# The channel mixer's seam: the first block's high and low parts summed once and kept for operands five and seven, with other places and orders of the passes

## The chip, the cores and the metric

The kernel runs on one core of a Trainium2 chip. The metric is the device time of one execution in microseconds (us), as the median of several runs. Engines are named as in the profile: PE (TensorE, matmuls), PEld (its weight loads), DVE (VectorE), ACT (ScalarE), POOL (GpSimd), SP (SyncE, which issues most transfers).

## The reference

Two encoder layers on 1024 tokens of width 1024; the mixers of tokens are a windowed attention in layer 0 and a gated linear recurrence in layer 1. The change touches only the channel mixer, which ends each layer:

```python
def conv_ffn(v, w_in, conv_w, conv_b, w_out):
    gate, up = jnp.split(v @ w_in, 2, axis=-1)
    hid = jax.nn.gelu(dwconv_centred(gate, conv_w, conv_b)) * up
    return hid @ w_out

def reference(x, mem, norm_g, ...):
    for layer in range(DEPTH):
        u = rmsnorm(h, norm_g[layer, 0])
        ...
        h = h + rmsnorm(y, norm_g[layer, 1])
        f = conv_ffn(rmsnorm(h, norm_g[layer, 2]), ffn_w_in[layer], ffn_conv_w[layer],
                     ffn_conv_b[layer], ffn_w_out[layer])
        h = h + rmsnorm(f, norm_g[layer, 3])
    return h
```

`v` is 1024 x 1024, `w_in` 1024 x 5632 (22 tiles of 128 gate columns and as many up columns), the convolution has width 3 along the tokens.

## The kernel before, in words

**Precision.** Each float32 operand is kept as two parts: a high part `h`, which ACT makes with a cast, and a low part `l`, which DVE makes as source minus `h` (function `split`; `nsplit` makes both with the sign turned). A product of two such operands is three matmuls per 128-deep slice: high by high, low by high, high by low.

**Seven products in place of eight.** The first matmul of the channel mixer (function `ffn`) sees its input `v` transposed as four blocks: channels 0-511 or 512-1023 by the 512 tokens of half `ti` or of half `tj`. For one tile `f` of 128 gate and 128 up columns the four block results (gate and up, each for both token halves) are formed from seven products of sums of blocks. `prod(k, ...)` runs product k: 4 slices by 3 matmuls, 12 matmuls of 128x128 by 128x512. The right-hand operands are `B[1]` to `B[7]`. `B[1]`, `B[2]`, `B[3]` and, at first, `B[5]` are the four blocks themselves, high and low (`uh`, `ul`). The others are sums, made once for each layer by `operands()`, in halves of 128x1024: x = block 1 - block 5 becomes operand five in place; x + block 3 gives operand six (`nsplit`); that minus block 1 gives operand seven; x (of six) minus block 2 gives operand four. Since a block lies there as high and low part, adding or subtracting it takes two DVE passes (helper `more`), so a layer's operands take 18 passes beside the splits: 6 for five, 4 each for six, seven and four.

The left-hand operands are sums of weight blocks, which transfers that add on the way into SRAM build (`load`: buffers `st`, `sx`, `sy`; the refill of `sy` waits until DVE has read the old one) and `weights` splits into `wh` and `wl`.

**The seam.** The operands aren't ready when the first matmul can start, so `first_units()` begins with tile 0 by plain products of the four blocks (`plain`, banks X, Y, V), and takes tiles 1 and 2 together: products 1 and 2 of both, then 5, 3, 6, 7, 4, each of both tiles before the next, in step with the operands as they get done. X, V and Y are accumulation banks, two of each; `su`, `s5`, `s` are copies of banks that ACT makes, and `u`, `g` are the up and gate results that `conv` takes. From tile 3 on the order is regular, and all operands lie there. The seam stands once in each layer: at about 560 to 640 us in layer 0, and at about 1985 to 2080 us in layer 1.

**What sets the order.** The kernel is written as a program of tiles; a scheduler puts the instructions on each engine's queue by priority, as their inputs come to be placed, and adds the semaphore waits. `tc.high_priority(AHEAD)` draws instructions forward by 2000 places, `tc.issue_after(x)` holds one back until x has been placed. Engines run their queues strictly in that order. Before the change only operand seven's passes are drawn forward.

## Time and profile before

| | us |
|---|---|
| median of 3 runs | 2633.48 |
| the runs | 2632.31, 2633.48, 2636.83 |
| profiled execution, its own time | 2636.21 |
| its span in the profile | 2634.4 |
| PE busy | 2594.2 (98%), 14372 matmuls |
| PEld busy | 2180.0 (83%) |
| DVE busy | 1753.5 (67%) |
| ACT busy | 1400.6 (53%) |
| POOL busy | 471.7 (18%) |

The profile shows one execution; the span is what lies between its first and last instruction. Busy PE time is not PE at its best: a matmul that starts late because the one before runs at a lower clock counts as busy. A timeline row reads: start (us), duration (us), engine, line, operation, output<-inputs, shape, count, and in square brackets the wait ahead of it and what ended the wait. L584 is the matmul in `mmk`, L85 the cast and L86 the subtraction of `split`, L607 and L608 those of `nsplit`, L663 the pass of `more`, L670 to L672 the passes of operand five, L808 and L824 the additions that make `u`, L788, L815 and L823 the copies `s`, `s5` and `su`.

### The profile page before, as it was taken

Reading aid. Unit: us, or ns where it says so; the run is one execution under the profiler, and the core shown is the slowest. Engines: PE = TensorE matmul, PEld = TensorE weight load, DVE = VectorE, ACT = ScalarE, POOL = GpSimd, SP = SyncE. Lnnn points to the kernel's source line nnn. Section 1 sums busy time; section 2 is a strip of 40 time slices with the busy share of each in tenths; the row PEclk is TensorE's granted clock in tenths of the full one; section 3 lists DMA queues with packets and bytes.
Section 4 is the critical chain, followed back from the end, with each engine's and each line's share of the span. In section 5 each row is a group of like instructions: output and inputs, shape, how many; then the busy total and the mean of one; then the engine's idle time right before and its main releaser. Section 6 shows DMA issues by size and latency. Waiting matters only on the chain.

```text
span 2634.4 us, 38871 instructions
## 1 busy us (share of the span) xinstructions
PE 2594.2 (98%) x14372; PEld 2180.0 (83%) x14372; DVE 1753.5 (67%) x2852; ACT 1400.6 (53%) x2534; POOL 471.7 (18%) x520
## 2 busy tenths in 40 slices
PE   8999999999999999999999999999999999999998
PEld 7988888888888888887888878888887788888887
DVE  6778777587656565487587575867657665656447
ACT  6667767445444444465465564646434444444453
POOL 0421110221111100032133131221311111110013
PEclk9999999999999999999999999999999999999999
DMA  9782232467877756683236241113337777775666
GB/s 357 248 191 47 75 114 61 130 186 189 214 198 200 199 155 221 220 274 124 85 122 172 81 112 41 61 49 97 122 112 200 199 198 199 203 200 170 202 210 232
DMA packets 195726, 425.92 MB, mean 162 GB/s; under 512 B 20048, under 2 KB 56272, under 8 KB 189904
## 3 DMA queue, kind: packets, MB, share of 16 engines
q1 hardware_dynamic: 161552, 324.06, 37.7%
q0 software_dynamic: 24544, 90.19, 16.5%
q10 hardware_dynamic: 9440, 9.19, 1.1%
q8 instruction: 113, 1.85, 0.3%
q14 instruction: 77, 0.63, 0.1%
HBM read 330.04 MB, written 116.39 MB: 169 GB/s over the span
## 4 chain that ended last, share of the span: by engine, by line
PE 90%; DVE 5%; DMA 2%; ACT 1%; issue 1%; POOL 0%; SPq 0%; DVEq 0%; ACTq 0%; POOLq 0%
PE X L584 29%; PE V L584 10%; PE pj L80 8%; PE pj L82 8%; PE pj L81 8%; PE Y L584 5%; PE pb L80 4%; PE pb L81 4%; PE pb L82 4%; PE po L1302 2%; PE pa L1221 1%; PE pt L386 1%; PE pu L1280 1%; PE po L390 1%; DMA sx<-in_ffw_dram 1%
## 5 line engine op out<-in xcount | busy, mean ns | idle before, releaser
L86 DVE TENSOR_TENSOR wl<-st,wh 128x1024 fp32r<-128x1024 f32 (+1 forms) x238 | 262.7, 1110 | 321.8 <-ACT wh L85 295.2
L85 ACT CAST wh<-st 128x1024 fp32r<-128x1024 f32 (+1 forms) x238 | 222.5, 936 | 286.5 <-PE X L584 179.8
L80 PE MATMUL pj<-uh,wh 128*128 128x512 f32 x512 | 204.1, 399 | 1.2 <-DVE q L1140 0.8
L584 PE MATMUL X<-wl,wh 128*128 128x512 f32 x528 | 204.9, 390 | 0.2 <-DVE wl L86 0.2
L584 PE MATMUL X<-wh,wl 128*128 128x512 f32 x528 | 204.9, 389 | 0.0
L81 PE MATMUL pj<-ul,wh 128*128 128x512 f32 x512 | 202.9, 396 | 0.0
L82 PE MATMUL pj<-uh,wl 128*128 128x512 f32 x512 | 202.3, 395 | 0.0
L584 PE MATMUL X<-wh 128*128 128x512 f32 x528 | 198.7, 390 | 0.6 <-DVE c L1014 0.6
L80 PE MATMUL pj<-wh,uh 128*128 128x384 f32 (+1 forms) x512 | 188.4, 369 | 1.0 <-DVE v L298 1.0
L82 PE MATMUL pj<-wh,ul 128*128 128x384 f32 (+1 forms) x512 | 187.2, 366 | 0.0
L81 PE MATMUL pj<-wl,uh 128*128 128x384 f32 (+1 forms) x512 | 186.9, 365 | 0.0
L76 DVE TENSOR_TENSOR wl<-st,wh 128x1024 fp32r<-128x1024 f32 (+1 forms) x90 | 115.5, 1288 | 24.1 <-ACT wh L75 22.8
L584 PE MATMUL V<-uh,wh 128*128 128x512 f32 x336 | 130.7, 389 | 0.0
L584 PE MATMUL V<-ul,wh 128*128 128x512 f32 x336 | 130.7, 389 | 0.0
L584 PE MATMUL V<-uh,wl 128*128 128x512 f32 x336 | 130.7, 389 | 0.0
L584 PEld LDWEIGHTS X<-wh 128*128 128x128 f32 x528 | 99.1, 188 | 21.7 <-issue 1.0
L584 PEld LDWEIGHTS X<-wl,wh 128*128 128x128 f32 x528 | 99.1, 188 | 21.3 <-DVE wl L86 0.7
L584 PEld LDWEIGHTS X<-wh,wl 128*128 128x128 f32 x528 | 99.1, 188 | 20.4
L75 ACT CAST wh<-st 128x1024 fp32r<-128x1024 f32 (+1 forms) x96 | 96.6, 1012 | 34.9 <-PE pj L81 20.0
L80 PEld LDWEIGHTS pj<-uh,wh 128*128 128x128 f32 x512 | 96.8, 189 | 20.4 <-DVE q L1140 1.2
L973 POOL TENSOR_TENSOR c<-c,g 128x512 f32<-128x512 f32 x24 | 43.2, 1818 | 389.4 <-PE X L584 320.1
L82 PEld LDWEIGHTS pj<-uh,wl 128*128 128x128 f32 x512 | 96.8, 189 | 19.3
(410 smaller groups left out, 7161.1 us busy)
## 6 DMA issues: line engine op xcount, KB each, us to landing
st<-hid SPq DMA_DIRECT2D x154, 256.0 KB, 3.3
st<-in_ffw_dram SPq DMA_DIRECT2D x108, 256.0 KB, 3.3
w2s<-in_ffw_dram POOLq DMA_DIRECT2D x24, 1024.0 KB, 8.5
st<-in_ffw_dram SPq DMA_DIRECT2D x46, 512.0 KB, 4.5
hid<-tt SPq DMA_DIRECT2D x88, 256.0 KB, 4.9
st<-w2s SPq DMA_DIRECT2D x88, 256.0 KB, 3.3
sx<-in_ffw_dram SPq DMA_DIRECT2D x84, 256.0 KB, 3.9
sy<-in_ffw_dram SPq DMA_DIRECT2D x42, 512.0 KB, 6.3
```

The costliest lines, as they stand in the source:

```text
L75: act.copy(h[:, :n], raw)
L76: (eng or dve).tensor_tensor(l[:, :n], raw, h[:, :n].bitcast(F32), op=ALU.subtract)
L80: pe.matmul(o, ah, bh, start=first, stop=False)
L81: pe.matmul(o, ah, bl, start=False, stop=False)
L82: return pe.matmul(o, al, bh, start=False, stop=last)
L85: act.copy(h, src)
L86: return dve.tensor_tensor(l, src, h.bitcast(F32), op=ALU.subtract)
L386: pe.transpose(tp[:, j, :], sm[:, j, c * P:(c + 1) * P], ident)
L390: pe.matmul(po, v[:, lo + c, :], pl, start=False, stop=c == hi - lo - 1)
L584: last = pe.matmul(o, x, y, start=first and i == 0, stop=i == len(ops) - 1, skip_group_check=not first)
L973: pool.tensor_tensor(y[q][:, t, :], y[q][:, t, :], g3[:, c], op=ALU.mult)
L1302: pe.matmul(po[:, c, :], x, y, start=i == 0, stop=i == len(ops) - 1)
```

## The change

In `operands`, the high and low part of block 1 are added once for each half into a buffer `whole`, which stays. Operand five becomes whole minus the two parts of block 5 (6 passes, as before), and operand seven one pass for each half, x - whole, in place of two: 16 passes in place of 18. The two sums take the two `tt` buffers until operand seven is split in place there; so the `u` of tile 2 moves from a `tt` buffer to the `g` buffer, and the `g` of both tiles take the `tt` buffers.

The rest sets orders. Operand six's splits are held until the last pass of tile 0's convolution has been placed (`wide[0]`, L616 after the change). Operand seven's subtractions are held until tile 1's `u<-Y` has been placed (`ups[0]`, now L814), its splits until tile 2's. Operand four's passes are held until the last low part of operand seven (`low7`). The splits of the second and third weight parts are held until operand five, and operand six, are split (`made5`). Lines move: L584 is now L583, the two lines of `split` are one, L85, `more` is L665, the passes of operand five L672 to L674, operand seven's L686, `u<-Y` L814, `u<-V` L831.

```diff
--- before.py
+++ after.py
@@ -82,8 +82,7 @@
         return pe.matmul(o, al, bh, start=False, stop=last)
 
     def split(h, l, src):
-        act.copy(h, src)
-        return dve.tensor_tensor(l, src, h.bitcast(F32), op=ALU.subtract)
+        return act.copy(h, src), dve.tensor_tensor(l, src, h.bitcast(F32), op=ALU.subtract)
 
     def rstd_of(pl, ss, n, count, tag):
         ms = pl.tile([P, n], F32, tag=tag + "ms", name=tag + "ms")
@@ -604,15 +603,18 @@
             B[k] = tuple(u2p.tile([P, 4, 512], F32R, name=f"u{k}{c}") for c in "hl")
         def nsplit(h, l_, src):
 
-            act.activation(h, src, AF.Copy, scale=-1.0)
-            dve.scalar_tensor_tensor(l_, src, -1.0, h.bitcast(F32), op0=ALU.mult, op1=ALU.subtract)
+            return (act.activation(h, src, AF.Copy, scale=-1.0),
+                    dve.scalar_tensor_tensor(l_, src, -1.0, h.bitcast(F32), op0=ALU.mult, op1=ALU.subtract))
+
+        wide = []
 
         def conv(f, g, u):
 
             c = fp.tile([P, T], F32, tag="c", bufs=3, name="c")
             act.activation(c, g, AF.Identity, bias=cb[:, f:f + 1], scale=ncw[:, f, 1:2])
             dve.scalar_tensor_tensor(c[:, 1:], g[:, :T - 1], ncw[:, f, 0:1], c[:, 1:], op0=ALU.mult, op1=ALU.add)
-            dve.scalar_tensor_tensor(c[:, :T - 1], g[:, 1:], ncw[:, f, 2:3], c[:, :T - 1], op0=ALU.mult, op1=ALU.add)
+            wide.append(dve.scalar_tensor_tensor(c[:, :T - 1], g[:, 1:], ncw[:, f, 2:3], c[:, :T - 1],
+                                                 op0=ALU.mult, op1=ALU.add))
             act.activation(c, c, AF.Gelu_apprx_tanh)
             dve.tensor_tensor(c, u, c, op=ALU.mult)
             return c
@@ -653,7 +655,7 @@
                 act.copy(u[:, m], up_)
             yield conv(f, g, u)
 
-        def operands(made5):
+        def operands(made5, ups):
 
             xs = [fp.tile([P, 2, 512], F32, tag="c", bufs=3, name="c") for _ in range(2)]
             tmp = lambda: fp.tile([P, 2, 512], F32, tag="tt", bufs=2, name="tt")
@@ -664,27 +666,31 @@
                     x = o
             def out_of(sp, k, kk, x):
                 return sp(half(B[k][0], kk), half(B[k][1], kk), x)
-            for kk, x in enumerate(xs):
-                q = tmp()
+            whole = [tmp() for _ in xs]
+            for kk, (x, q) in enumerate(zip(xs, whole)):
                 f32 = lambda t, c: half(t[c], kk).bitcast(F32)
-                dve.tensor_tensor(x, f32(B[1], 0), f32(B[5], 0), op=ALU.subtract)
-                dve.tensor_tensor(q, f32(B[1], 1), f32(B[5], 1), op=ALU.subtract)
-                dve.tensor_tensor(x, x, q, op=ALU.add)
+                dve.tensor_tensor(q, f32(B[1], 0), f32(B[1], 1), op=ALU.add)
+                dve.tensor_tensor(x, q, f32(B[5], 0), op=ALU.subtract)
+                dve.tensor_tensor(x, x, f32(B[5], 1), op=ALU.subtract)
             for kk, x in enumerate(xs):
                 made5.append(out_of(split, 5, kk, x))
             yield
             for kk, x in enumerate(xs):
                 more(x, x, B[3], kk, ALU.add)
-                out_of(nsplit, 6, kk, x)
+            for kk, x in enumerate(xs):
+                with tc.issue_after(wide[0].ins):
+                    made5.append(out_of(nsplit, 6, kk, x))
+            yield
+            for kk, (x, q) in enumerate(zip(xs, whole)):
+                with tc.high_priority(AHEAD), tc.issue_after(ups[0].ins):
+                    dve.tensor_tensor(q, x, q, op=ALU.subtract)
+            for kk, q in enumerate(whole):
+                with tc.high_priority(AHEAD), tc.issue_after(ups[1].ins):
+                    low7 = out_of(split, 7, kk, q)[1]
             yield
             for kk, x in enumerate(xs):
-                q = tmp()
-                with tc.high_priority(AHEAD):
-                    more(q, x, B[1], kk, ALU.subtract)
-                    out_of(split, 7, kk, q)
-            yield
-            for kk, x in enumerate(xs):
-                more(x, x, B[2], kk, ALU.subtract)
+                with tc.issue_after(low7.ins):
+                    more(x, x, B[2], kk, ALU.subtract)
                 out_of(split, 4, kk, x)
             yield
 
@@ -789,8 +795,8 @@
 
 
             tiles = (1, 2)
-            made5 = []
-            pl, opd = plain(0), operands(made5)
+            made5, ups = [], []
+            pl, opd = plain(0), operands(made5, ups)
             next(pl)
             raws = {f: load(f) for f in tiles}
             gens = {f: weights(raws.pop(f)) for f in tiles}
@@ -804,16 +810,17 @@
                 start(us[f])
                 y = psx.tile([P, 512], F32, tag="Y", name="Y")
                 prod(2, operand(us[f], 2), y, True)
-                us_[f] = fp.tile([P, T], F32, tag="u" if f == 1 else "tt", bufs=1 if f == 1 else 2, name="u")
-                dve.tensor_tensor(us_[f][:, ti], y, s[1], op=ALU.add)
-            with tc.issue_after(made5[-1].ins):
+                us_[f] = fp.tile([P, T], F32, tag="u" if f == 1 else "g", bufs=1, name="u")
+                ups.append(dve.tensor_tensor(us_[f][:, ti], y, s[1], op=ALU.add))
+            with tc.issue_after(made5[1][0].ins), tc.issue_after(made5[1][1].ins):
                 more_of()
             for f in tiles:
                 vs[f] = psx.tile([P, 512], F32, tag="V", name="V")
                 prod(5, operand(us[f], 5), vs[f], True)
                 s5[f] = fp.tile([P, 512], F32, tag="s5" if f == 1 else "s1", bufs=1, name="s5")
                 act.copy(s5[f], vs[f])
-            more_of()
+            with tc.issue_after(made5[3][0].ins), tc.issue_after(made5[3][1].ins):
+                more_of()
             next(opd)
             for f in tiles:
                 prod(3, operand(us[f], 3), vs[f], False)
@@ -828,7 +835,7 @@
             gen = weights(raws.pop(3))
             for f, x in zip(tiles, X):
                 prod(7, operand(us[f], 7), x, False, f == 1)
-                gs[f] = gtile() if f == 1 else fp.tile([P, T], F32, tag="tt", bufs=2, name="tt")
+                gs[f] = fp.tile([P, T], F32, tag="tt", bufs=2, name="tt")
                 act.copy(gs[f][:, tj], x)
                 dve.tensor_tensor(gs[f][:, tj], gs[f][:, tj], s5[f], op=ALU.add)
                 ops.append(next(gen))
```

The order of DVE (VectorE) in layer 1 around operand seven, before; `tt` is operand seven ahead of its split, `c` in `more` (L663) operand four, u7l and u4l the low parts:

```order
L86 TENSOR_TENSOR wl<-sy,wh 128x1024
L808 TENSOR_TENSOR u<-Y,s_19291 128x512
L808 TENSOR_TENSOR u<-Y,s_19321 128x512
L663 TENSOR_TENSOR tt<-c,uh 128x1024
L663 TENSOR_TENSOR tt<-tt,ul 128x1024
L663 TENSOR_TENSOR c<-c,uh 128x1024
L86 TENSOR_TENSOR wl<-st,wh 128x512
L824 TENSOR_TENSOR u<-V,su 128x512
L86 TENSOR_TENSOR u7l<-tt,u7h 128x1024
L663 TENSOR_TENSOR c<-c,ul 128x1024
L663 TENSOR_TENSOR tt<-c,uh 128x1024
```

And with the change:

```order
L85 TENSOR_TENSOR wl<-sy,wh 128x1024
L814 TENSOR_TENSOR u<-Y,s_19287 128x512
L686 TENSOR_TENSOR tt<-c,tt 128x1024 x2
L814 TENSOR_TENSOR u<-Y,s_19317 128x512
L85 TENSOR_TENSOR u7l<-tt,u7h 128x1024
L85 TENSOR_TENSOR wl<-st,wh 128x512
L831 TENSOR_TENSOR u<-V,su 128x512
L85 TENSOR_TENSOR u7l<-tt,u7h 128x1024
L665 TENSOR_TENSOR c<-c,uh 128x1024 x2
L665 TENSOR_TENSOR c<-c,ul 128x1024 x2
L831 TENSOR_TENSOR u<-V,su 128x512
L85 TENSOR_TENSOR wl<-st,wh 128x512
```

Both halves of operand seven are now subtracted and split ahead of every pass of operand four; before, a pass of operand four stood between the halves' passes. Ahead of these rows, the last pass of tile 0's convolution and both of operand six's low parts now stand ahead of both `wl<-sy` passes; before, one of those stood ahead of them. The two kept sums `tt<-uh,ul` (L672) stand ahead of the last `wl` and `ul` passes of the layer's norm, where before nothing of the operands stood.

ACT (ScalarE) in layer 1 at the same place, before; u7h and u4h are the high parts:

```order
L85 CAST u7h<-tt 128x1024
L823 COPY su<-X 128x512
L85 CAST wh<-st 128x512
L85 CAST u4h<-c 128x1024
L85 CAST u7h<-tt 128x1024
L85 CAST u4h<-c 128x1024
L832 COPY g<-X 128x512
```

And with the change:

```order
L85 CAST u7h<-tt 128x1024
L821 COPY s_19370<-V 128x512
L830 COPY su<-X 128x512
L85 CAST wh<-st 128x512
L85 CAST u4h<-c 128x1024
L839 COPY tt<-X 128x512
L85 CAST u4h<-c 128x1024
```

The u7h row of the first fence is the first half's, with the second half's behind the first u4h; in the second fence the u7h row is already the second half's, ahead of the copy `su`; both u4h casts now stand behind tile 2's `wh<-st` cast.

PE in layer 1 where tile 2's first product (X_19308 before, X_19304 now) begins behind tile 1's, with buffer numbers, before; V and `qin` belong to tile 0's plain product:

```order
L584 MATMUL X_19278<-uh_77,wl_19237 128x512
L584 MATMUL X_19308<-uh_77,wh_19240 128x512
L584 MATMUL X_19308<-ul_78,wh_19240 128x512
L584 MATMUL V_19085<-uh_77,qin0_18436 128x512
L584 MATMUL Y_19086<-uh_77,wh_19031 128x512
L584 MATMUL Y_19293<-uh_77,wh_19236 128x512
```

And with the change:

```order
L583 MATMUL X_19304<-uh_77,wh_19236 128x512
L583 MATMUL X_19304<-ul_78,wh_19236 128x512
L583 MATMUL X_19304<-uh_77,wl_19237 128x512
L583 MATMUL X_19304<-uh_77,wh_19236 128x512
L583 MATMUL X_19304<-ul_78,wh_19236 128x512
L583 MATMUL X_19304<-uh_77,wl_19237 128x512
```

The rows left out with the change are six more of the product's 12 matmuls and then V; before, two of the 12 stood ahead of V, and the other ten later.

## The prediction

> **What bounds the kernel now.** First the page's head and the table of busy times, then the table of waits of TensorE (PE), because only time in which PE stands still or runs slowly can be won here: the change moves passes of DVE and ACT and leaves all matmuls in.
>
> ```profile
> span 2634.4 us, 38871 instructions
> PE 2594.2 (98%) x14372; PEld 2180.0 (83%) x14372; DVE 1753.5 (67%) x2852; ACT 1400.6 (53%) x2534; POOL 471.7 (18%) x520
> ...
> engine line waited for: us in total, times, longest us
> PE X L584 <- ACT u7h L85: 3.8, 1, 3.8
> PE X L584 <- ACT wh L85: 0.9, 1, 0.9
> PE X L584 <- DVE u7l L86: 0.5, 1, 0.5
> PE V L584 <- ACT uh L85: 0.2, 1, 0.2
> ```
>
> PE is busy for 98%. The rows with L584 are all the waits that it has in the two channel mixers, 5.4 us, and all four lie in the seams. Two of them are for operand seven: 3.8 us in layer 1, 0.5 us in layer 0. So the timeline of PE there, layer 1 first, then layer 0, then one window with the granted clock (0.86, behind the busy times of PE, PEld, DVE, ACT and POOL):
>
> ```profile
> 2039.09 0.39 PE L584 MATMUL X<-u7h,wl 128*128 128x512 f32 x1
> 2039.32 0.39 PE L584 MATMUL X<-u7h,wh 128*128 128x512 f32 x1
> 2039.54 0.39 PE L584 MATMUL X<-u7l,wh 128*128 128x512 f32 x1
> 2039.77 0.39 PE L584 MATMUL X<-u7h,wl 128*128 128x512 f32 x1
> 2043.98 0.80 PE L584 MATMUL X<-u7h,wh 128*128 128x512 f32 x1 [3.83 <-ACT u7h L85]
> 2044.58 0.63 PE L584 MATMUL X<-u7h,wl 128*128 128x512 f32 x1
> 2045.00 0.63 PE L584 MATMUL X<-u7h,wh 128*128 128x512 f32 x1
> ...
> 2048.84 0.39 PE L584 MATMUL X<-u4h,wh 128*128 128x512 f32 x1
> ...
> 610.73 0.39 PE L584 MATMUL X<-u7h,wl 128*128 128x512 f32 x1
> ...
> 614.90 0.98 PE L584 MATMUL X<-u7l,wh 128*128 128x512 f32 x3 [0.45 <-DVE u7l L86]
> ...
> 616.64 0.40 PE L584 MATMUL X<-u4h,wh 128*128 128x512 f32 x1
> ...
> 2037.00:2049.00 12.00, 8.18 (x29) 6.33 (x29) 10.89 (x12) 4.82 (x6) 2.63 (x3) 0.86 0.61 131
> ```
>
> Undisturbed starts stand (2039.77 - 2039.09) / 3 = 0.227 us apart. From 2039.77 to 2048.84 PE starts 15 matmuls, 15 x 0.227 = 3.40 us of work in 9.07: **5.67 us** lost. 3.98 of it is the wait, and 1.69 comes behind it, where starts are 0.43 apart (2044.58, 2045.00) and the window's clock falls to 0.86. In layer 0, 21 starts from 610.73 to 616.64 are 4.76 us in 5.91: **1.15 us**. The most that operand seven can give is 6.82 us.
>
> [...]
>
> Why operand seven is late, the queue of DVE shows:
>
> ```profile
> 2029.22 0.68 DVE L808 TENSOR_TENSOR u<-Y,s 128x512 f32<-128x512 f32 x1
> ...
> 2033.56 1.22 DVE L663 TENSOR_TENSOR c<-c,uh 128x1024 f32<-128x1024 f32 x1
> ...
> 2038.17 1.22 DVE L663 TENSOR_TENSOR tt<-c,uh 128x1024 f32<-128x1024 f32 x1
> ...
> 2041.64 1.22 DVE L663 TENSOR_TENSOR tt<-tt,ul 128x1024 f32<-128x1024 f32 x1
> 2042.77 1.22 DVE L663 TENSOR_TENSOR c<-c,uh 128x1024 f32<-128x1024 f32 x1
> ...
> 2042.89 1.04 ACT L85 CAST u7h<-tt 128x1024 fp32r<-128x1024 f32 x1 [3.56 <-DVE tt L663]
> ```
>
> DVE works without a pause from 2031 to 2046. The second half of operand seven (tt, 2038.17 and 2041.64) queues behind passes of operand four (c, from 2033.56), and its cast ends at 2043.93, where PE goes on. It is the order on DVE, not its amount of work, that PE waits for.
>
> **The change part by part.** *Passes.* Operand five takes 6 passes as before, seven 2 in place of 4, by the kept sums: 16 in place of 18 in each layer. A pass takes 1.22 us, and a start follows 1.13 behind another (2041.64 to 2042.77). So DVE loses 2 x 1.13 = 2.3 us per layer, worth nothing in itself off PE's path.
>
> *The kept sums* now stand ahead of the seam on DVE. In layer 0, and behind it in layer 1, DVE has holes:
>
> ```profile
> 571.88 0.69 DVE L86 TENSOR_TENSOR ul<-pt,uh 128x512 fp32r<-128x512 f32 x1 [2.92 <-ACT uh L85]
> ...
> 1993.87 1.28 DVE L86 TENSOR_TENSOR ul<-pt,uh 128x512 fp32r<-128x512 f32 x2
> 2001.50 1.23 DVE L86 TENSOR_TENSOR wl<-st,wh 128x1024 fp32r<-128x1024 f32 x1 [6.35 <-ACT wh L85]
> ...
> 1997.32 1.03 PE L117 MATMUL pt<-ident,nu 128*128 128x128 f32 x8
> ```
>
> Two sums, 2.27 us, fit into 2.92 and 6.35. In layer 1 they push the two ul halves from 1993.87-1995.15 to 1997.42; the transposes pt that need their bank stand at 1997.32, but now with four more X matmuls ahead, at 1998.2. Cost 0, cover 0.8 us; without that cover it would be up to 2.27.
>
> *Seven ahead of four.* From 2029.22 on DVE now does: u (0.6), both subtractions (2.27), u, u7l, wl, u, u7l, then four passes of operand four. So both tt are whole at 2029.8 + 2.4 = 2032.2, ACT has the second u7h by about 2034.6 (behind wh, su and the first u7h), and DVE the second u7l by 2036.3. PE, which now does the second tile's V product behind the first tile's seven, asks for u7h's second half at about 2036.2: 1.6 us to spare, where it was 4 late. I take the whole 6.82 us back.
>
> *What is late next* is operand four. PE comes to it at 2048.84 - 5.67 = 2043.2 (2043.5 with the loss below). Its four passes now stand from 2036.3 to 2040.8 on DVE, but its casts stand on ACT behind one that waits for PE:
>
> ```profile
> 2037.70 0.62 ACT L85 CAST wh<-st 128x512 fp32r<-128x512 f32 x1 [1.04 <-PE V L584]
> 2038.28 1.05 ACT L85 CAST u4h<-c 128x1024 fp32r<-128x1024 f32 x1
> ```
>
> That V product of the second tile now ends at about 2040.3, the wh cast at 2040.9, u4h at 2041.9, u4l (1.22, behind u and wl) at 2043.5, and the second matmul of operand four wants it at 2043.7. The two meet within 0.2 us; layer 0 has the same order and the same distance. Bounds: 0, and 2.0 for both seams (each cast behind the wait late by one more cast, 1.05); I take 0.3, nearer to 0, since the rows leave it just on time.
>
> *The second tile's first product* stands whole ahead of V in PE's queue in layer 1 (12 matmuls; before, 2):
>
> ```profile
> 2000.42 1.04 ACT L85 CAST wh<-st 128x1024 fp32r<-128x1024 f32 x1 [7.51 <-DMA st<-in_ffw_dram]
> 2001.52 0.50 PE L584 MATMUL X<-uh,wh 128*128 128x512 f32 x1 [0.88 <-ACT wh L85]
> 2001.85 0.40 PE L584 MATMUL X<-ul,wh 128*128 128x512 f32 x1
> 2002.49 0.50 PE L584 MATMUL V<-uh,qin 128*128 128x512 f32 x1 [0.24 <-ACT uh L85]
> ```
>
> The wait of 0.88 stays: as many matmuls stand ahead of it, and the load is issued as before. The third matmul now reads wl, which DVE ends at 2001.50 + 1.23 = 2002.73; V went on at 2002.49. Cost 0.3 us; bounds 0 (another order of ends) and 0.5.
>
> *The other orders*, issue constraints, the u of tile two in the buffer of g and both g in tt cost PE nothing that a row shows: their passes keep their number and PE has no other wait here. The refill of the shared weights is later; that is the third rival.
>
> Sum: -6.82 + 0.3 + 0.3 = **-6.2 us**. The profiled execution took 2636.21 us (span 2634.4), 2.7 above the median of the runs shown, 2633.48, and inside their range (2632.31 to 2636.83). From its time the sum makes 2630.0; from the median, which is what is asked for, 2633.5 - 6.2 = 2627.3.
>
> **Rivals.**
> *Operand four is late by as much as a cast on ACT.* The bound above: 2.0 in place of 0.3 gives -4.5 us, 2629.0. For it: the wait at ACT's head and the margin of 0.2. Against: PE now has other matmuls (V, Y of tile three) mixed in there.
>
> *The slow stretch is not in the median run.* The 1.69 us behind the wait hang on the clock falling to 0.86. If a run of median time has the wait without it, the gain is 6.2 - 1.7 = 4.5 us: 2629.0 too. For it: the profiled run lies 2.7 above the median. Against: the wait of 3.83 is itself long, and the spread may come from elsewhere. [...]
>
> *Slower: the refill of the shared weights.* The wl<-sy pass, which frees the buffer sy for tile three's load, now stands behind STT and both u6l passes on DVE, 1.19 + 2 x 1.13 = 3.5 us later, and SP, POOL and POOL follow in a chain:
>
> ```profile
> 2023.31 0.33 SPq L700 DMA_DIRECT2D sy<-in_ffw_dram  x1
> 2032.70 0.89 POOL L703 DMA_DIRECT2D sy<-sx  x1 [1.10 <-DVE tt L663]
> 2038.37 0.88 POOL L704 DMA_DIRECT2D sy<-sy  x1 [4.79 <-DMA sy<-sx]
> 2051.53 1.05 ACT L85 CAST wh<-sy 128x1024 fp32r<-128x1024 f32 x1 [0.66 <-PE X L584]
> ...
> DMA to landing us min/median/max: 3.3/5.1/9.6
> ```
>
> Moved by 3.5, the last add starts at 2041.9 and lands, 5.1 later, at 2047.0; ACT wants it at 2051.53 - 5.4 = 2046.1 and has the copies that free PE's bank X behind it, with some 3 us until PE asks for that bank. From 4 us of further delay PE waits one for one; with all three transfers at 9.6 it is 13.5 later, PE waits some 9.5, and 9.5 - 6.2 makes it 3 slower; slower by over 5.3 us needs two such seams: 2640. Against it: the queue rows keep gaps, and two passes are saved.
>
> *The change does not bring seven forward*: then only the 0.3 is left, 2633.8. The order on DVE speaks against it: nothing of operand four stands ahead of u7l.
>
> **How the numbers follow.** Forecast 0.52; operand four late 0.15; no slow stretch in the median 0.22; seven not forward or part of it 0.06; slower 0.05. What can be told from no change is 0.2%, 5.3 us, so faster means below 2628.2. The forecast's own spread (its costs at 0 to 2.5 together, and a median that moves by about 1) runs from 2625 to 2630; of its 0.52 I count 0.41 below 2628.2, and 0.10 of the two cases at 2629.0 (each could be half as large). Faster 0.51, same 0.44, slower 0.05. Predicted 2627.3; range 2623 to 2633: below, 6.82 without costs (2626.7) and some 4 for the spread of the runs, which lie 4.5 apart; above, the two rivals at 2629.0 and the same 4.
>
> **What would show it.** Right: no wait of PE for u7h or u7l in either seam, clock 1.00 in the windows of layer 1, both tt<-c,tt passes back to back behind the first u<-Y. The wait for wh at the second tile's first product still there, near 0.9, with one of about 0.6 for wl behind it. Waits of PE for u4h, u4l or the copy of X: below 0.3 each if my sum holds, about 1 if the first rival does. A wait for wh<-sy or for X's bank in tile three would show the slower case. The forecast is wrong if the waits are gone and the time is not: then the median runs never held them in full.

## The result, and the profile after

The changed kernel takes 2629.75 us in the median of 16 runs (2626.55 to 2635.04), the kernel before, in the same comparison, 2634.07 us (16 runs). The ratio is 0.9979 with a 95% interval of 0.9973 to 0.9986: some 5.5 us faster, between 3.7 and 7.1. The forecast was 6.2 us and 2627.3.

The profiled execution took 2631.85 us. The head of its page, and all waits of PE between 1975 and 2100 us (engine, line, what it waited for: us in total, times, longest); the same view between 560 and 660 us is empty:

```profile
span 2630.1 us, 38871 instructions
PE 2593.0 (99%) x14372; PEld 2179.7 (83%) x14372; DVE 1747.6 (66%) x2848; ACT 1400.2 (53%) x2534; POOL 470.2 (18%) x520
```

```profile
PE X L583 <- ACT wh L85: 2.0, 1, 2.0
PE X L583 <- DVE wl L85: 0.5, 1, 0.5
```

DVE has four instructions fewer: the two saved passes in each layer. No wait for operand seven is left, and none for operand four. The timeline of DVE in layer 1, then ACT, then PE, shows why:

```profile
2030.37 2.35 DVE L686 TENSOR_TENSOR tt<-c,tt 128x1024 f32<-128x1024 f32 x2
2032.64 0.68 DVE L814 TENSOR_TENSOR u<-Y,s 128x512 f32<-128x512 f32 x1
...
2035.58 1.21 DVE L85 TENSOR_TENSOR u7l<-tt,u7h 128x1024 fp32r<-128x1024 f32 x1
2036.71 2.35 DVE L665 TENSOR_TENSOR c<-c,uh 128x1024 f32<-128x1024 f32 x2
...
2042.71 1.22 DVE L85 TENSOR_TENSOR u4l<-c,u4h 128x1024 fp32r<-128x1024 f32 x1
...
2034.46 1.05 ACT L85 CAST u7h<-tt 128x1024 fp32r<-128x1024 f32 x1
...
2041.11 0.62 ACT L85 CAST wh<-st 128x512 fp32r<-128x512 f32 x1 [4.17 <-PE V L583]
2041.63 1.04 ACT L85 CAST u4h<-c 128x1024 fp32r<-128x1024 f32 x1
...
2036.15 0.39 PE L583 MATMUL X<-u7h,wh 128*128 128x512 f32 x1
...
2044.53 0.39 PE L583 MATMUL X<-u4l,wh 128*128 128x512 f32 x1
```

Both halves of `tt` are whole at 2032.72, the second u7h at 2035.51, and PE is in operand seven from 2036.15 without a pause; its fifth matmul, at 2036.15 + 4 x 0.227 = 2037.06, is the first that reads the second u7h. Operand four's u4h is ready at 2042.67 and u4l at 2043.93, 0.6 us ahead of the matmul that reads it.

What is left is at the start of layer 1's seam, where the second tile's first product waits for its weights and then runs slowly. PE's timeline there, and the windows view of two stretches (the seventh figure is the granted clock):

```profile
1998.36 0.39 PE L583 MATMUL X<-uh,wl 128*128 128x512 f32 x1
2000.75 0.50 PE L583 MATMUL X<-uh,wh 128*128 128x512 f32 x1 [2.00 <-ACT wh L85]
...
2002.01 0.50 PE L583 MATMUL X<-uh,wl 128*128 128x512 f32 x1 [0.53 <-DVE wl L85]
...
2003.47 0.63 PE L583 MATMUL X<-uh,wh 128*128 128x512 f32 x1
2003.89 0.63 PE L583 MATMUL X<-ul,wh 128*128 128x512 f32 x1
...
2005.99 0.40 PE L583 MATMUL V<-uh,qin 128*128 128x512 f32 x1
```

```profile
2000.50:2006.00 5.50, 4.73 (x13) 3.43 (x14) 5.27 (x6) 2.15 (x5) 0.86 (x1) 0.69 1.03 291
2035.00:2050.00 15.00, 15.00 (x67) 12.08 (x66) 13.49 (x15) 7.36 (x11) 2.71 (x4) 1.00 0.80 183
```

From 1998.36 to 2005.99 PE starts 13 matmuls, 13 x 0.227 = 2.95 us of work in 7.63: 4.7 us lost. In the kernel before, this place lost 1.7 (the waits of 0.88 and 0.24 and a slower start behind each). A run of starts 0.43 us apart, nearly twice the 0.227 between undisturbed ones, is called a slow stretch below; the granted clock of 0.69 in the first window shows it (0.51 from 2002.6 to 2006.0 alone, 0.50 from 2043.9 to 2047.2 in the first profile of before).

### The profile page after: what moved, and what is told of

The parts are those of the page before. It is cut to its first block, busy times and chain, and to the rows that moved or that the text cites. A ratio compares the mean times of both kernels' runs of the same rounds, so it can differ in the third digit from the quotient of the medians.

```text
span 2630.1 us, 38871 instructions
## 1 busy us (share of the span) xinstructions
PE 2593.0 (99%) x14372; PEld 2179.7 (83%) x14372; DVE 1747.6 (66%) x2848; ACT 1400.2 (53%) x2534; POOL 470.2 (18%) x520
## 4 chain that ended last, share of the span: by engine, by line
PE 92%; DVE 4%; DMA 2%; ACT 1%; issue 1%; POOL 0%; SPq 0%; ACTq 0%; DVEq 0%; POOLq 0%
PE X L583 30%; PE V L583 11%; PE pj L80 8%; PE pj L82 8%; PE pj L81 8%; PE Y L583 5%; PE pb L80 4%; PE pb L82 4%; PE pb L81 4%; PE po L1309 2%; PE pt L385 1%; PE pa L1228 1%; PE pu L1287 1%; PE po L389 1%; PE pt L116 1%
## 5 line engine op out<-in xcount | busy, mean ns | idle before, releaser
L85 DVE TENSOR_TENSOR wl<-st,wh 128x1024 fp32r<-128x1024 f32 (+1 forms) x238 | 262.8, 1111 | 319.4 <-ACT wh L85 301.6
L85 ACT CAST wh<-st 128x1024 fp32r<-128x1024 f32 (+1 forms) x238 | 222.4, 936 | 290.5 <-PE X L583 178.0
L583 PE MATMUL X<-wl,wh 128*128 128x512 f32 x528 | 204.9, 390 | 0.2 <-DVE wl L85 0.2
L583 PE MATMUL X<-wh,wl 128*128 128x512 f32 x528 | 204.9, 389 | 0.0
L583 PE MATMUL X<-wh 128*128 128x512 f32 x528 | 198.7, 390 | 0.6 <-DVE c L1021 0.6
L583 PE MATMUL V<-uh,wh 128*128 128x512 f32 x336 | 130.8, 389 | 0.0
L583 PE MATMUL V<-ul,wh 128*128 128x512 f32 x336 | 130.7, 389 | 0.0
L583 PE MATMUL V<-uh,wl 128*128 128x512 f32 x336 | 130.7, 389 | 0.0
L583 PEld LDWEIGHTS X<-wh 128*128 128x128 f32 x528 | 99.1, 188 | 21.7 <-issue 1.0
L583 PEld LDWEIGHTS X<-wl,wh 128*128 128x128 f32 x528 | 99.1, 188 | 21.1 <-DVE wl L85 0.7
L583 PEld LDWEIGHTS X<-wh,wl 128*128 128x128 f32 x528 | 99.1, 188 | 20.6
```

The costliest lines, as they stand in the source:

```text
L85: return act.copy(h, src), dve.tensor_tensor(l, src, h.bitcast(F32), op=ALU.subtract)
L583: last = pe.matmul(o, x, y, start=first and i == 0, stop=i == len(ops) - 1, skip_group_check=not first)
```

## The experiments

All runs were compared with runs of the kernel before on the same chip. Beside the time stands a measure from the one profile that each kernel left: how much longer than 0.2275 us the starts of PE lie apart, summed over all that are more than 0.26 apart, from 555 to 660 and from 1975 to 2100 us of the profile. It is PE's loss in the two seams. The names are those of the runs: order_only has the orders without the kept sums, sums_only the sums without the constraints, ups_only only the two constraints on operand seven, gate_only operand four held behind seven, buf_only the buffers alone, sums_behind the sums later, and a1 stands for the early load.

| kernel | median us (runs) | ratio to before, 95% | PE's loss in the seams, us |
|---|---|---|---|
| before, first profile | 2634.07 (16) | | 8.9 |
| before_again | 2636.00 (12) | 1.0004 (0.9994 to 1.0013) | 11.1 |
| changed | 2629.75 (16) | 0.9979 (0.9973 to 0.9986) | 5.4 |
| after_again | 2628.89 (11) | 0.9976 (0.9967 to 0.9985) | 4.9 |
| order_only | 2627.20 (8) | 0.9978 (0.9968 to 0.9988) | 2.5 |
| sums_only | 2638.32 (11) | 1.0013 (1.0004 to 1.0022) | 12.0 |
| ups_only | 2628.64 (7) | 0.9975 (0.9965 to 0.9985) | 3.4 |
| gate_only | 2634.00 (11) | 0.9999 (0.9990 to 1.0008) | 8.1 |
| buf_only | 2636.51 (11) | 1.0013 (1.0004 to 1.0022) | 12.5 |
| sums_behind | 2627.92 (11) | 0.9977 (0.9968 to 0.9986) | 2.4 |
| before_a1 | 2634.90 (11) | 0.9998 (0.9990 to 1.0007) | 9.1 |
| a1_first | 2624.84 (5) | 0.9963 (0.9951 to 0.9976) | 0.8 |
| a1_again | 2626.24 (5) | 0.9965 (0.9953 to 0.9977) | 0.9 |
| order_a1 | 2629.63 (11) | 0.9983 (0.9974 to 0.9992) | 2.5 |

Against the mean of the two profiles of before, 10.0, the loss explains every ratio within about 3 us; so the effect lies in the seams, as far as these times can tell.

### Both kernels once more

No edit. For the changed kernel:

> The changed kernel once more. Theory E (the wait for tile 2's first weights and the slow stretch behind it come in every run): a wait of 0.9 to 2.0 us for wh, one near 0.5 for wl, then 6 to 10 starts that are 0.43 apart. Rival F (the slow stretch is there in some runs only): the same waits, but no or few starts above 0.3. No wait for u7h, u7l, u4h or u4l above 0.3 in either case. Time 0.1 to 0.3% below before.

Waits of 1.76 and 0.53 us came again, with a slow stretch behind them from about 2001 to 2004.2, and no wait for operands seven or four. For the kernel before:

> The kernel before once more. Theory K (the slow stretch behind the 3.8 us wait is part of what the change takes away in every run): wait for u7h 3.7 to 3.9, then at least 4 starts that are 0.43 apart. Rival L (it is there in some runs only): the same wait with starts 0.23 apart behind it, so that operand seven is worth 1.5 less than in the first profile. Waits of 0.5 for u7l in layer 0 and of 0.8 to 1.1 for wh in layer 1 in either case.

The first seam stall was longer this time, the wait for u7h shorter. PE's timeline:

```profile
2002.88 0.50 PE L584 MATMUL X<-uh,wh 128*128 128x512 f32 x1 [1.34 <-ACT wh L85]
...
2003.86 0.55 PE L584 MATMUL V<-uh,qin 128*128 128x512 f32 x1 [0.24 <-ACT uh L85]
...
2045.78 0.80 PE L584 MATMUL X<-u7h,wh 128*128 128x512 f32 x1 [2.64 <-ACT u7h L85]
```

Theory K holds in these profiles as to the slow stretch: it is there, and it is longer (13 starts 0.43 apart, to 2051.92; in the first profile 6). But the wait for u7h was 2.64, not the 3.7 to 3.9 that both theories expected. PE had lost 3.7 us at the seam's start (1.6 of waits and a slow stretch), 2.0 more than in the first profile, and waited 1.2 less at operand seven: the two stalls aren't independent. PE won nothing by that here: with the longer slow stretch behind it, operand seven cost 5.8 us in layer 1, against 5.7 in the first profile. The next run shows the dependence more cleanly.

### The early load, on the kernel before

```diff
-            raws = {f: load(f) for f in tiles}
+            a1s = {f: first_load(f) for f in tiles}
+            raws = {f: load(f, a1s[f]) for f in tiles}
```

`first_load` allocates the staging buffer of a tile's first weights and issues their load; `load` no longer does.

> The kernel before, with tile 2's first weights loaded early as in the faster version of the changed kernel, and nothing else. Theory C (the load is a loss of its own): the waits of 0.9 for wh and 0.2 for uh at the seam's start go, 1.0 to 1.5 us faster than before; the waits of 3.8 and 0.5 for operand seven stay. Rival M (PE then only comes earlier to operand seven): the wait for u7h grows by what the start has saved, 4.5 to 5 us, and the time stays within 0.5 us of before.

All waits of PE in layer 1's seam:

```profile
PE X L584 <- ACT u7h L85: 5.4, 1, 5.4
```

PE at its first matmul into Y and where operand seven goes on; the first row is the kernel before, the others the kernel with the early load:

```profile
1991.30 0.47 PE L584 MATMUL Y<-uh,wh 128*128 128x512 f32 x1
```

```profile
1989.19 0.47 PE L584 MATMUL Y<-uh,wh 128*128 128x512 f32 x1
...
2041.91 0.80 PE L584 MATMUL X<-u7h,wh 128*128 128x512 f32 x1 [5.38 <-ACT u7h L85]
```

Rival M is right in direction: the waits at the start are gone, and the wait for u7h has grown from 3.8 to 5.4 (it said 4.5 to 5), by what the start had saved. Operand seven goes on 52.7 us after the first matmul into Y in both profiles (1991.30 to 2043.98 before), whether PE lost 1.7 us at the seam's start or nothing. In before_again, with 3.7 lost, it was 53.6; whether the larger loss held the chain up isn't shown. The ratio of the times, 0.9998, agrees, though its interval alone would leave room for the 1.0 to 1.5 us of theory C. In these two profiles operand seven comes when the chain on DVE and ACT has made it, and since that chain ends last, the 1.7 us that PE lost ahead of it were free.

### The early load, on the changed kernel

The same edit on the changed kernel, run twice.

> The changed kernel, but tile 2's first weight load is issued directly behind tile 1's first load, and takes the staging buffer that tile 1's last load took; no other edit. Theory C (what the changed kernel still loses at the start of layer 1's seam is this load: wait for wh 2.0, for wl 0.5, then 8 starts that are 0.43 apart, 1.6 us): all three are gone, 4.1 us less than the changed kernel's profiled run, 2.5 to 4.5 less in the median. Rival D (V and the transposed halves are late anyway, as the wait of 0.24 for uh before V shows): the wait moves to V<-uh, 1.5 to 2 us of it stay, gain below 2 us.

> The changed kernel with the early load once more, for its interval: 3.5 to 5 us faster than the changed kernel (0.9955 to 0.997 of before), no wait of PE in the channel mixers' seams above 0.3.

SP, ACT and PE of the first of them (tile 2's load is the second of the two on SP; its wh cast is the row of ACT; the last row is V behind the whole product), then PE's windows over the seam, of the kernel before, the changed one and this one:

```profile
1971.35 9.57 SPq L700 DMA_DIRECT2D st<-in_ffw_dram  x2
...
1988.07 1.06 ACT L85 CAST wh<-st 128x1024 fp32r<-128x1024 f32 x1
...
1996.94 0.40 PE L583 MATMUL X<-uh,wh 128*128 128x512 f32 x1
...
1998.99 0.40 PE L583 MATMUL V<-uh,qin 128*128 128x512 f32 x1
```

```profile
1975.00:2080.00 105.00, 100.06 (x442) 81.64 (x442) 78.59 (x87) 48.99 (x66) 16.18 (x20) 0.98 0.74 198
```

```profile
1975.00:2080.00 105.00, 102.47 (x453) 83.58 (x452) 75.67 (x85) 48.23 (x66) 16.15 (x20) 0.98 0.75 201
```

```profile
1975.00:2080.00 105.00, 105.00 (x472) 86.44 (x471) 79.00 (x85) 53.37 (x71) 16.43 (x20) 1.00 0.76 199
```

Theory C holds: the weights are cast at 1988, PE runs from the first product into V and on, and is busy for all of the 105 us with a granted clock of 1.00. On the changed kernel the edit is worth 4.0 to 4.6 us by the seams' loss, where on the kernel before it was worth nothing. The two ratios, 0.9963 and 0.9965 of before (some 9.5 us), lie 3 to 4 us below those of the changed kernel, with intervals that overlap a little; this is the fastest version of the study.

### The orders without the kept sums

```diff
-                dve.tensor_tensor(q, f32(B[1], 0), f32(B[1], 1), op=ALU.add)
-                dve.tensor_tensor(x, q, f32(B[5], 0), op=ALU.subtract)
-                dve.tensor_tensor(x, x, f32(B[5], 1), op=ALU.subtract)
+                dve.tensor_tensor(x, f32(B[1], 0), f32(B[5], 0), op=ALU.subtract)
+                dve.tensor_tensor(q, f32(B[1], 1), f32(B[5], 1), op=ALU.subtract)
+                dve.tensor_tensor(x, x, q, op=ALU.add)
...
-                    dve.tensor_tensor(q, x, q, op=ALU.subtract)
+                    more(q, x, B[1], kk, ALU.subtract)
```

> The changed kernel's orders and buffers, with the 18 passes of before: block 1 is not summed ahead, operand seven takes four passes again. Theory A (the order on DVE is what PE waited for): no wait of PE for u7h or u7l above 0.7 us in either seam, against 3.8 and 0.5 before, since both halves of operand seven still stand ahead of operand four. Rival B (the two saved passes are what counts): the wait for u7h comes back with 2 us or more. Under A the two passes that are not saved (2.27 us on DVE) should show one step later, at operand four: its last low part, which had 0.2 to 0.6 us to spare, comes 1 to 2 us late in layer 1, so the kernel is 1 to 2.5 us slower than the changed one and still 2 to 4 faster than before.

PE's waits in layer 1's seam (layer 0's has none):

```profile
PE Y L583 <- ACT wh L85: 0.5, 1, 0.5
PE V L583 <- ACT wh L85: 0.5, 1, 0.5
PE X L583 <- ACT u4h L85: 0.2, 1, 0.2
```

Theory A holds: no wait for operand seven with all 18 passes. Where operand four is due there are waits of 1.2 us, 0.2 of them for operand four itself and the rest for weights cast beside it on ACT. The kernel was expected to be slower than the changed one and is not: its seams lose 2.4 to 2.9 us less. At the start of layer 1's seam it has no wait, since the scheduler puts V and Y of the plain tile ahead of tile 2's first product, and its weights are cast by then:

```profile
1996.49 1.05 ACT L85 CAST wh<-st 128x1024 fp32r<-128x1024 f32 x1 [2.10 <-DMA st<-in_ffw_dram]
...
1996.23 0.40 PE L583 MATMUL V<-uh,qin 128*128 128x512 f32 x1
```

This order at the start isn't due to the missing sums alone: the kernel before has none either and puts two matmuls of tile 2's product ahead of V, and the runs with the buffers alone and with operand four held back, told of below, have V first as well. The scheduler moves this place with edits made elsewhere. So by the waits the sums save some 1.2 us at operand four; what they cost at the start this run can't tell.

### The sums without the constraints

The changed kernel with every `issue_after` that it brought taken out again (here the pair at operand seven; each half's subtraction and split then stand together again, in one loop):

```diff
-                with tc.high_priority(AHEAD), tc.issue_after(ups[0].ins):
+                with tc.high_priority(AHEAD):
                     dve.tensor_tensor(q, x, q, op=ALU.subtract)
...
-                with tc.high_priority(AHEAD), tc.issue_after(ups[1].ins):
-                    low7 = out_of(split, 7, kk, q)[1]
+                    out_of(split, 7, kk, q)
```

> The changed kernel with the kept sums, 16 passes and the new buffers, but without every constraint on the order (operand six, seven and four and the two weight splits are held behind nothing new). The passes of seven are then drawn forward ahead of both u<-Y additions. Theory A (the constraints matter): u<-Y of tile 1 comes some 4 us later, the copy s of tile 2 on ACT waits for it, and PE waits 2 to 6 us in a place where it waited for nothing in the changed kernel (for u7h, V or Y); time within 2 us of before. Rival B (sums and buffers are enough): seams as in the changed kernel, time within 1 us of it.

PE's largest waits over both seams:

```profile
PE X L583 <- ACT s L789: 3.4, 2, 1.7
PE X L583 <- ACT su L824: 2.5, 3, 1.0
PE X L583 <- ACT wh L85: 2.1, 1, 2.1
PE V L583 <- ACT s L816: 0.7, 1, 0.7
```

Slower than before: 1.0013. Operand seven is early, but its passes, drawn forward, push `u<-Y` back; the copies s and su come late, and PE waits for the banks that these have to empty. Theory A's mechanism holds, and more strongly than it said: 6.6 us of such waits over both seams in place of 2 to 6, and 3.4 us slower than before (1.1 to 5.8) where it said within 2.

### The sums with only the two constraints on operand seven

The kernel just told of, with `issue_after(ups[0])` and `issue_after(ups[1])` put back.

> The changed kernel with the kept sums and the new buffers, and of all constraints only the two that hold operand seven's subtractions and splits behind the u<-Y additions. Theory H (these two are what the kernel with the sums alone lacked): no wait for the copies s and su; the second half's u7l, with three more passes ahead of it on DVE, comes 3.4 us later than in the changed kernel, where it had 1.6 to spare, so a wait of 1 to 2 us for u7l in layer 1; 0.5 to 2.5 us slower than the changed kernel and faster than before. Rival N (the constraints on operands six and four are needed too): waits for su, s or u4 of over 2 us come back.

PE's waits in layer 1's seam (layer 0's has one of 0.3 us):

```profile
PE X L583 <- ACT wh L85: 1.2, 1, 1.2
PE X L583 <- DVE wl L85: 0.5, 1, 0.5
```

As fast as the changed kernel (0.9975). Theory H is right about the waits for s and su, and too dark about u7l: the wait of 1 to 2 us didn't come, and the kernel isn't slower than the changed one. Of all constraints these two are enough, as far as an interval of 2.6 us to each side can tell.

### The buffers alone, and the order alone

The kernel before, with the two buffers exchanged and nothing else:

```diff
-                us_[f] = fp.tile([P, T], F32, tag="u" if f == 1 else "tt", bufs=1 if f == 1 else 2, name="u")
+                us_[f] = fp.tile([P, T], F32, tag="u" if f == 1 else "g", bufs=1, name="u")
...
-                gs[f] = gtile() if f == 1 else fp.tile([P, T], F32, tag="tt", bufs=2, name="tt")
+                gs[f] = fp.tile([P, T], F32, tag="tt", bufs=2, name="tt")
```

> The kernel before with nothing but the two buffers exchanged: tile 2's u in the g buffer, both g in the tt buffers. 18 passes, no constraint on the order. Rival G (the buffer was the cause): both halves of seven can be made at once, waits for u7h gone. Theory H (the buffer frees seven, but with no constraint the passes drawn forward push both u<-Y additions back, as in the kernel with the sums alone, where PE waited 3.4 us for the copy s and 2.5 for su): waits for s and su of 4 to 8 us in the two seams together, 2 to 7 us slower than before. Both may hold: then the buffers are needed and the constraints too.

PE's waits over both seams:

```profile
PE X L584 <- ACT su L823: 3.4, 4, 1.8
PE X L584 <- ACT u7h L85: 2.3, 1, 2.3
PE X L584 <- ACT s L788: 1.2, 1, 1.2
```

Theory H holds: waits of 4.6 us for s and su, and slower than before. Rival G's waits for u7h aren't gone: one of 2.3 us stays, since a pass of operand four still stands between operand seven's on DVE. So the buffers alone are not enough. The kernel before, with operand four held behind operand seven and nothing else:

```diff
-                    out_of(split, 7, kk, q)
+                    low7 = out_of(split, 7, kk, q)
...
-                more(x, x, B[2], kk, ALU.subtract)
+                with tc.issue_after(low7.ins):
+                    more(x, x, B[2], kk, ALU.subtract)
```

> The kernel before with one constraint: operand four's passes are held until the last low part of operand seven. No kept sums, and the buffers of before, in which tile 2's u holds one of the two tt buffers. Theory A (only the order on DVE was wrong): the waits for operand seven go, no other comes, 5 to 7 us faster than before. Rival G (the buffer was the cause: the second half of operand seven has no tt buffer until the first is split, so seven's passes run one half behind the other and only pull operand four back): waits for seven fall under 1 us, but waits of 2 to 6 us for u4h or u4l come in layer 1; within 3 us of before.

PE's three largest waits over both seams:

```profile
PE X L584 <- ACT u7h L85: 1.6, 2, 1.1
PE X L584 <- ACT u4h L85: 1.4, 2, 0.7
PE Y L584 <- ACT wh L85: 1.0, 2, 0.5
```

No gain (0.9999). The wait for operand seven shrinks to 1.6 us over both seams, and the rest turns into smaller waits for operand four and for weights cast beside it on ACT. Rival G is right about the time and the direction; its waits of under 1 us for seven and of 2 to 6 for operand four were both off. With tile 2's u in one of the two `tt` buffers, operand seven's halves can only be made one behind the other, so its passes and operand four's can't all be early. The two constraints that hold operand seven behind `u<-Y` weren't tried with these buffers, but there is nothing left for them to do: on DVE both `u<-Y` already stand ahead of operand seven's first pass in this kernel (2028.30, 2029.63 and 2030.24 in layer 1) and in the kernel before. It takes the free buffers, and with them the two constraints.

### The sums later

```diff
+                with tc.issue_after(turned[-1].ins) if turned else nullcontext():
                     dve.tensor_tensor(q, f32(B[1], 0), f32(B[1], 1), op=ALU.add)
```

`turned` holds the last low part of the norm's transposes.

> The changed kernel, with its two kept sums held until the last low part of the norm's transposes, so that they no longer stand ahead of those on DVE in layer 1; PE's order at the seam's start is then that of before (two matmuls of tile 2's first product ahead of V, where the changed kernel has twelve). Theory I (the loss at the start, 4.1 us in the changed kernel's profile, comes with that order, which the sums ahead of the transposes bring about): the wait for wh falls to 0.5 to 1.2, no wait for wl, no slow stretch; 2 to 4 us faster than the changed kernel. Rival C' (the load alone decides): wait for wh near 1.8 still, and within 1 us of the changed kernel. Making the sums later should cost nothing at operand five.

PE's waits in layer 1's seam (layer 0's has none):

```profile
PE X L584 <- ACT wh L85: 1.0, 1, 1.0
...
PE V L584 <- ACT uh L85: 0.2, 1, 0.2
```

The profile looks as theory I said: two matmuls of tile 2's product ahead of V as before, a wait of 1.0, none for wl there, no slow stretch, and 2.5 to 3.0 us less loss than in the two profiles of the changed kernel. In time the gain is not to be told from nothing: 0.9977 against 0.9979 and 0.9976. And the loads say that C' is right about the wait. Tile 2's first load and its cast, in the kernel before (the cast, at 2000.42, is shown in the prediction) and in the changed one:

```profile
1994.07 0.42 SPq L697 DMA_DIRECT2D st<-in_ffw_dram  x1
```

```profile
1992.17 0.42 SPq L703 DMA_DIRECT2D st<-in_ffw_dram  x1
...
1999.65 1.04 ACT L85 CAST wh<-st 128x1024 fp32r<-128x1024 f32 x1 [8.63 <-DMA st<-in_ffw_dram]
```

From issue to cast it is 6.35 us and 7.48, and the waits were 0.88 and 2.00: in both the wait is this time less 5.47. The same holds within 0.01 in all seven profiles in which PE comes to this product ahead of V without the early load, whether two or twelve of its matmuls stand there (here 6.52 us, and a wait of 1.05). The order decides only what comes next, a wait of 0.53 for wl or of 0.24 for uh: 0.3 us.

### The orders without the sums, with the early load

The edits of the orders without the sums, and of the early load, together.

> The new orders and buffers with 18 passes, and tile 2's first weights loaded early. Theory J (the two saved passes are worth only what was seen without them in layer 1: waits of 0.5, 0.2 and 0.5 near operand four and the weights behind it): these waits stay, about 1.2 us in all with nothing at the seam's start, so it is 1 to 2 us slower than the changed kernel with the early load and the same as the new orders alone. Rival B (the saved passes matter more as soon as nothing else waits): over 2.5 us slower than the changed kernel with the early load.

The waits near operand four are the same as without the early load (0.5, 0.4 and 0.2), and PE's loss is the same 2.5: as J said, the early load has nothing to win there. By the loss it is 1.7 us behind the kernel with sums and early load, by the ratios 5 (0.9983 against 0.9963 and 0.9965, with intervals that touch at 0.9974 to 0.9976). Which of J and B is right in size stays open.

## Why the prediction was right, point by point

**What bounded the kernel.** PE's waits in the seams: right. The kernels' times follow PE's loss there, within 3 us. One reading was incomplete: line L584 has two more waits in the kernel before, 0.6 and 0.2 us at 2596 and 2608, in the second matmul; they lie outside the seams.

**Operand seven, 6.8 us taken back.** The waits went as forecast, and the margin of the second u7h was 2037.06 - 2035.51 = 1.55 us, forecast 1.6. The size held too: wait and slow stretch together lost 6.8 and 6.9 us in the two profiles of before, and nothing of that is left. What the prediction didn't see is that the stall hangs on what stands ahead of it: in the kernel before the wait for u7h was 3.83, 2.64 or 5.4 us, where PE had lost 1.7, 3.7 or nothing at the seam's start.

**"It is the order on DVE, not its amount of work".** Right about the amount: 18 passes do as well as 16, as long as the early load isn't added. About the order it is half the cause. Held in order alone, without the buffer, nothing is won; and drawn forward without the constraints on `u<-Y`, seven makes the kernel slower. The prediction did not see that tile 2's u held the buffer that the second half of seven needed.

**The kept sums, worth nothing in themselves.** Right for the changed kernel within what can be told. With the early load on both sides they save 1.7 us by the loss and some 5 by the ratios, so they count for something once nothing else waits; how much stays open.

**Operand four, 0.3 us (0 to 2.0).** No wait was seen; the low part came 0.6 us ahead.

**The step that was mis-sized: "the second tile's first product", 0.3 us (0 to 0.5).** It said that the wait of 0.88 stays and some 0.3 comes for wl. Measured were 2.00 and 0.53, then 1.76 and 0.53, with a slow stretch behind them each time: 4.7 us lost in place of 1.7 in the first pair of profiles, 4.3 in place of 3.7 in the second, so 3.0 and 0.6 and not 0.3. The 0.3 for the order was itself right. Two other things were missed, and with it they make up the 3.0 of the first pair: 1.1 because "the load is issued as before" doesn't fix when it is cast (6.4 and 6.8 us from issue to cast in the two profiles of before, 7.5 and 7.2 in those of the changed kernel), and 1.6 for the slow stretch, which the first profile of before didn't have at this place and the second had. Whether the change makes the load longer stays open: with the same sums ahead it was 6.7 in the kernel with two constraints, and without them 7.0 and 7.1 with the buffers alone and with operand four held back, so it may be chance.

**Why the total came out all the same.** From the first pair of profiles the loss in the seams fell by 3.5 us, from the second by some 6; the measured 5.5 lies between. That it lies near the forecast 6.2 is in part luck: had every execution gone as in the first pair, the gain would have been 3.5, just under the measured interval. Where operand seven's stall is gone the start's stall counts in full (the early load then took 4.0 to 4.6 us off PE's loss), since no later wait absorbs it any more; in the kernel before the wait for seven was the last in line (3.83 us, and 5.38 with the early load).

**The rivals.** The slow stretch behind operand seven was in both profiles of before, longer in the second, and in the one with the early load, so the second rival falls as far as three profiles tell. That a run of median time could have the wait without it, its chance of 0.22, was the author's estimate; only at the seam's start did the stretch come in one profile of before and not in the other. The first, operand four late, falls with the 0.6 us to spare. For the third, the refill of the shared weights: its last add now starts at 2042.95 at the latest, but the cast that needs it waited for PE and not for the transfer:

```profile
2042.95 0.86 POOL L710 DMA_DIRECT2D sy<-sy  x1 [0.49 <-DMA sy<-sx]
...
2049.70 1.05 ACT L85 CAST wh<-sy 128x1024 fp32r<-128x1024 f32 x1 [2.88 <-PE X L583]
```

## What to carry to other kernels

Here the stalls of one engine in a row didn't simply add: as long as a later chain on other engines ended last, an earlier stall of PE was paid out of the later one (with the 1.7 us at the start gone, the wait for u7h was 5.38 us in place of 3.83). With the last one taken away, the earlier one, that was free, was charged in full; look at it first, since here its cure, a load issued one place earlier, was worth nothing before the change (0.9998) and 4.0 to 4.6 us of PE's time after it. And when passes are drawn forward, ask which buffer they need and whose small pass they now stand ahead of (with the sums alone PE waited 6.6 us for the copies behind such passes). Last, when a wait for a load differs between two profiles, compare the load's own time first: here that explained the wait to 0.01 us, and the order of the matmuls did not.

## What the runs showed of the hardware that was not expected

A slow stretch also came behind gaps far shorter than the 3.83 us of the prediction. In before_again two gaps of 1.34 and 0.24 us were followed by 8 starts 0.43 apart; in the changed kernel gaps of 2.00 and 0.53 by 7. In the kernels with the sums alone (2.06 and 0.53) and with two constraints (1.23 and 0.53) no start was slow. So it was no fixed price of a gap. Two of the stretches lasted 3.4 us (2004.20 to 2007.61 in before_again, 2002.61 to 2005.99 in the changed kernel) and one 6.1 (2045.78 to 2051.92, behind the wait for u7h in before_again); with the buffers alone, where gaps of 1.79, 2.34 and 1.22 us followed each other closely, slow starts came for some 8 us (2033.73 to 2042.31). What decides whether a stretch comes, and how long it lasts, was not shown.
